# Where a mixture-of-experts stage sums its outputs: in the tokens themselves, or in two tiles of their own

## The chip, the core and the metric

The kernel runs on one core of a Trainium2 chip. The core has a matrix engine (PE, whose weight loads are shown apart as PEld), a vector engine (DVE), a scalar engine (ACT), a general one (POOL), and SP, which here issues nearly all DMAs. The metric is the time of one execution on the device in microseconds (us), as the median of several runs. A profile is one further execution, recorded by the hardware.

## The reference

Two encoder layers over 512 tokens of 1024 float32 values, each layer an attention block followed by a mixture of experts, and a final norm. The change lies in the mixture. Each of 16 experts picks its 64 best tokens by softmax affinity, runs a gated MLP over them, weighs its outputs with the affinity, and all outputs are added to the tokens from which they came:

```python
def expert_choice_ffn(xn, w_router, w_gate, w_up, w_down):
    aff = jax.nn.softmax((xn @ w_router).astype(jnp.float32), axis=-1)
    g, idx = lax.top_k(aff.swapaxes(1, 2), cap)          # cap = 64
    xs = xn[bidx, idx]
    hid = jax.nn.silu(jnp.einsum('becd,edf->becf', xs, w_gate)) * jnp.einsum('becd,edf->becf', xs, w_up)
    y = jnp.einsum('becf,efd->becd', hid, w_down) * g[..., None].astype(xn.dtype)
    return jnp.zeros_like(xn).at[bidx, idx].add(y)
...
        h = h + expert_choice_ffn(rms_norm(h, ffn_norm[l]), w_router[l], w_gate[l], w_up[l], w_down[l])
```

Every expert reads the tokens as they were before any expert's output was added. The result must therefore be summed somewhere while the unchanged tokens are still wanted.

## The kernel before, in words

The tokens stand in SBUF in two tiles h[0] and h[1] (columns 0 to 511 and 512 to 1023), four groups of 128 tokens each. The experts are worked off in eight pairs (e = 0, 2, ... 14), an expert of a pair on each half of the 128 output rows. For a pair the kernel:

- makes a one-hot matrix `oh` on DVE that says which token goes to which of 128 places (`one_hot`);
- gathers: PE multiplies the tokens with `oh`, which gives the pair's tokens already transposed, in eight blocks `k` of 128 columns. DVE evicts them times the norm's gain into `xs`;
- forms gate products (`og`, bank tag `in`), then up products (bank tag `S`), `expert_mm` at L1195; in the middle of the gate stage it also adds the half left over from the pair before (`rest`) and makes the affinities and the transposed one-hot matrix `G` (`places`);
- applies the gate, transposes the hidden values, forms the two halves of the down products (n = 0, 1), splits each half into a high and a low f32r part (`weighted`), and scatters it back through `G` (`combine`, L1364), whose result DVE adds into h (L1365).

The last three pairs (`tail` = 3) form only their first down half at once; the second halves come after pair 7, when the next layer's input products are already being mixed in.

Three devices keep the tokens readable in the kernel before. Pairs 0 and 1 gather from h itself (`gather`, L1223): exact f32 products of 128 columns. Pair 0's two down halves are not added to h but kept in a tile `hold` until pair 2 (`held`). After pair 1's gather h is split into an f32r high part `hh` and a low part `hl` (`token_parts`, ACT and POOL, four big tiles), and from these the later pairs gather in rounds (`gather_round`, L1236): pairs 2 and 3, 4 and 5, 6 and 7 together, 256 columns at a time, once with `hh` and once with `hl`. The first round stands before pair 2; the other two stand in pairs 3 and 5, around the transposes of the hidden values.

The order on PE in this stage is the order in which the code is written, since nearly all of its matmuls are `pinned`. DVE, ACT and POOL follow a scheduler. SP sends the weights in the order of use. All big tiles (tokens, parts, sums, held halves, gathered tokens of the rounds, weights `ew` of 1 MB each) come out of one pool of 25 buffers of 1 MB; a weight tile is sent when a buffer is free for it and the eighth DMA before it has landed.

Of the kernel before, what the change touches and what calls it, by code (L numbers as in the profile page):

```python
# [9 lines left out]
F32 = mybir.dt.float32  # L10
F32R = mybir.dt.float32r
# [5 lines left out]
P = 128  # L17
# [44 lines left out]
def build(tc, x, w_in, w_uq, w_ukv, w_out, w_gate, w_up, w_down, pv, wr, cst, nab, fin, out):  # L62
    nc = tc.nc
    ctx = ExitStack()
    with ctx:
# [303 lines left out]
        for L in range(DEPTH):  # L369
# [833 lines left out]
            ROUNDS = ((0,), (1,), (2, 3), (4, 5), (6, 7))  # L1203
            round_of = {pair: r for r in ROUNDS for pair in r}

            def token_parts(j):

                hh, hl = (big(n, F32R).rearrange("p (t d) -> p t d", t=NT) for n in ("hh", "hl"))
                for t in range(NT):
                    pinned(nc.scalar.activation(hh[:, t], h[j][:, t], AF.Copy))  # L1210
                    sub(nc.gpsimd, hl[:, t], h[j][:, t], hh[:, t])
                for x, part in zip(st.setdefault("parts", ([], [])), (hh, hl)):
                    x.append(part)
# [15 lines left out]
            def gather_round(oh, n, k0, m):  # L1229

                pg = p_t()[:, :m * n * P].rearrange("p (k s) -> p k s", k=m)
                for k in range(m):
                    cs = slice((k0 % 4 + k) * P, (k0 % 4 + k + 1) * P)
                    for t in range(NT):
                        for x in st["parts"]:
                            pinned(nc.tensor.matmul(pg[:, k], x[k0 // 4][:, t, cs], oh[:, t],  # L1236
                                                    start=(t == 0 and x is st["parts"][0]),
                                                    stop=(t == NT - 1 and x is st["parts"][1])))
                for i in range(n):
                    nc.vector.tensor_tensor(st["xs"][:, i, k0:k0 + m], pg[:, :, i * P:(i + 1) * P],  # L1240
                                            gains(k0, m), op=ALU.mult)

            def hidden(e, gate_w=(), up_w=(), ahead=None, before=None, then=None):
# [24 lines left out]
                if ahead:  # L1268
                    i = len(late)
                    if i % 4 == 0:  # L1270
                        st["G"] = big("G", F32R)
                    G = st["G"][:, i % 4 * 512:i % 4 * 512 + 512]
                else:

                    G = sm("qn" if pair in (1, 2) else "kn", F32R)

                def places():

                    pA = p_q()
                    for t in range(NT):  # L1280
                        pinned(nc.tensor.matmul(pA[:, :NEXP + 1], oh[:, t] if whole else oh[:, t].bitcast(F32),
                                                affr[:, t], start=(t == 0), stop=(t == NT - 1)))
# [6 lines left out]
                    nc.vector.tensor_copy(G, pG if whole else pG.bitcast(F32))  # L1289
# [24 lines left out]
                n = len(round_of.get(pair + 1, ())) if pair and pair == round_of[pair][-1] else 0  # L1314
                if n:
                    oh_n = one_hot(spool.tile([P, 2 * 512], F32R, name=nm("oh"), tag="oh", bufs=1), e + 2, 2 * n)
# [11 lines left out]
                def next_round(k0, k1):  # L1328
                    if k0 == 0:
                        st["xs"] = big("xs").rearrange("p (i k s) -> p i k s", i=2, k=KD)  # L1330
                    for k in range(k0, k1, 2):
                        gather_round(oh_n, n, k, 2)
                    if k1 == KD:
                        st["oh"] = oh_n
# [12 lines left out]
                if n and not whole:  # L1347
                    next_round(KD - 2, KD)
# [10 lines left out]
            def combine(n, y, G, banks, cs):  # L1359

                for t in range(NT):
# [3 lines left out]
                    nc.vector.tensor_tensor(h[n][:, t, cs], h[n][:, t, cs], o, op=ALU.add)  # L1365

            def half_then(n, ws, G, asl, hT, before=None, bank=p_s, banks=(p_q, p_t, p_t, p_o), cs=slice(0, 512),
                          held=False):
# [6 lines left out]
                if held:  # L1375
                    if n == 0:
                        st["hold"] = big("hold")
                    y = st["hold"][:, n * 512:(n + 1) * 512]
                    act(y, oy, asl)

                    def later():

                        yh, yl = sm("sb", F32R), sm("sb", F32R)
                        act(yh, y)
                        sub(nc.vector, yl, y, yh)
                        return lambda: combine(n, (yh, yl), G, banks, cs)
                    return later
# [3 lines left out]
            gate_w, rest, held = gate0, None, []  # L1391
            for e in range(0, NEXP - 2 * tail, 2):
                then = None
                if e == 4:
                    def then():
                        held.pop(0)()()
                p = hidden(e, gate_w, up0 if e == 0 else (), before=rest, then=then)
                down_w = down0 if e == 0 else [down_half(e, n) for n in range(2)]
                gate_w = [weights(w_gate, 2, k, 2) for k in range(0, KD, 2)] if e == 0 else ()
                if e == 0:  # L1400
                    held += [half_then(n, down_w[n], *p, held=True) for n in range(2)]
                    continue
                if e == 2:
                    token_parts(0)
                rest = half_then(0, down_w[0], *p, held.pop(0)() if e == 4 else None)
                if e == 2:
                    token_parts(1)
                rest = half_then(1, down_w[1], *p, rest)
                if e == 2:
                    st["gather"]()  # L1410
# [194 lines left out]
```

## Time and profile before

| | us |
|---|---|
| median of 3 runs | 1532.53 (1530.0 to 1533.62) |
| the profiled execution, its own time | 1528.89 |
| its span in the profile | 1527.1 |
| PE busy | 1444.4 (95%) |
| PE weight loads busy | 854.5 (56%) |
| DVE busy | 598.1 (39%) |
| ACT busy | 367.4 (24%) |
| POOL busy | 237.7 (16%) |

The span is what the profile covers of the execution's own time; 1.8 us lie around it. An f32 product stands in the records as two matmuls, an f32r product as one. A matmul's end in the records is modelled and lies behind the start of the next one, so what a piece of PE's work takes is read from start to start. Layer 0's first gather starts at 307.12, layer 1's at 1065.02.

### The profile page before, as it was taken

The numbers are of one execution on the slowest core, as the hardware profiler recorded it, in microseconds if no ns is written. First come the engines' busy times: TensorE is split into PE (matmuls) and PEld (weight loads), VectorE is DVE, ScalarE is ACT, GpSimd is POOL, SyncE is SP. The second block draws the span as 40 slices with busy tenths as digits, with TensorE's granted clock in tenths as the row PEclk, the third lists the DMA queues.
The fourth block names the chain that finished last, engine by engine and source line by source line (L and its number), as shares of the span: only waits on it lengthen the run. The fifth ranks groups of instructions, "written<-read, shape, count | busy, mean of one in ns | idle before, by whom it ended". The sixth has DMA issues, their size and how long they took to land.

```text
span 1527.1 us, 21209 instructions
## 1 busy us (share of the span) xinstructions
PE 1444.4 (95%) x8262; PEld 854.5 (56%) x8262; DVE 598.1 (39%) x1519; ACT 367.4 (24%) x949; POOL 237.7 (16%) x339
## 2 busy tenths in 40 slices
PE   9999899999999999987999998998999999999886
PEld 8987777644444433532489877675444434344323
DVE  6767675710223212210376577657102222221113
ACT  4434645300200000001134346452101000000002
POOL 3532442000200000000124235320002000000002
PEclk9999999999999999999999999999999999999998
DMA  6122263789999999999811123547899999999995
GB/s 202 51 71 78 70 203 139 303 327 414 376 415 421 421 421 421 421 421 418 342 56 44 52 77 111 163 192 300 341 380 409 417 420 420 421 421 422 421 421 232
DMA packets 80436, 444.99 MB, mean 291 GB/s; under 512 B 7761, under 2 KB 23633, under 8 KB 32465
## 3 DMA queue, kind: packets, MB, share of 16 engines
q1 hardware_dynamic: 76688, 438.40, 72.0%
q0 software_dynamic: 3648, 5.24, 1.6%
q8 instruction: 65, 1.06, 0.3%
q14 instruction: 35, 0.28, 0.1%
HBM read 436.28 MB, written 2.10 MB: 287 GB/s over the span
## 4 chain that ended last, share of the span: by engine, by line
PE 76%; DMA 15%; DVE 6%; ACT 2%; issue 1%; POOL 0%; DVEq 0%; SPq 0%; ACTq 0%; POOLq 0%
PE S L1195 19%; PE in L1195 14%; DMA ew<-in_w_gate_dram 5%; DMA ew<-in_w_up_dram 5%; PE in L161 5%; PE in L163 5%; PE in L162 5%; PE tr L155 5%; PE o L297 4%; DMA ew<-in_w_down_dram 4%; PE tr L1236 2%; PE tr L1223 2%; PE tr L1364 2%; PE trq L1364 1%; PE trq L1009 1%
## 5 line engine op out<-in xcount | busy, mean ns | idle before, releaser
L1195 PE MATMUL S<-ew,PT 128*64 128x512 f32 x960 | 214.0, 595 | 2.4 <-DMA ew<-in_w_down_dram 2.4
L1195 PE MATMUL S<-ew,xs 128*64 128x512 f32 x768 | 173.3, 594 | 11.9 <-DMA ew<-in_w_up_dram 11.9
L1195 PE MATMUL in<-ew,xs 128*64 128x512 f32 x768 | 172.6, 595 | 5.9 <-DMA ew<-in_w_gate_dram 5.9
L1321 DVE SCALAR_TENSOR_TENSOR sb<-S,rsl,sb 128x512 f32<-128x512 f32 x32 | 24.0, 751 | 302.2 <-PE S L1195 302.2
L1195 PEld LDWEIGHTS S<-ew,PT 128*64 128x64 f32 x960 | 67.1, 137 | 133.2 <-issue 127.2
L1195 PEld LDWEIGHTS S<-ew,xs 128*64 128x64 f32 x768 | 56.7, 137 | 126.5 <-issue 100.4
L1195 PEld LDWEIGHTS in<-ew,xs 128*64 128x64 f32 x768 | 54.3, 137 | 109.3 <-issue 97.0
L146 POOL TENSOR_SCALAR wh<-wraw 128x384 fp32r<-128x384 f32 (+2 forms) x40 | 36.9, 942 | 360.0 <-DMA ew<-in_w_down_dram 300.0
L1310 ACT ACTIVATE sb<-in,rsl 128x512 f32<-128x512 f32 x32 | 21.8, 687 | 245.5 <-PE in L1195 198.1
L161 PE MATMUL in<-wh,hT 128*128 128x256 f32 (+1 forms) x256 | 77.6, 304 | 0.3 <-ACT cut L143 0.3
L162 PE MATMUL in<-wl,hT 128*128 128x256 f32 (+1 forms) x256 | 77.6, 303 | 0.0
L163 PE MATMUL in<-wh,hT 128*128 128x256 f32 (+1 forms) x256 | 77.4, 303 | 0.0
L1195 PE MATMUL in<-ew,PT 128*64 128x512 f32 (+1 forms) x352 | 73.9, 559 | 0.0
L1365 DVE TENSOR_TENSOR h<-h,trq 128x512 f32<-128x512 f32 (+1 forms) x31 | 20.8, 671 | 130.2 <-PE trq L1364 130.2
L155 PE MATMUL tr<-c,sb 128*128 128x128 f32 x324 | 55.1, 284 | 7.5 <-DVE sb L1321 4.2
L1345 ACT ACTIVATE PT<-tr 128x512 f32<-128x512 f32 x24 | 14.3, 597 | 187.6 <-PE tr L155 187.6
L146 POOL TENSOR_SCALAR sb<-sb,cut 128x512 f32<-128x512 f32 (+2 forms) x64 | 43.0, 672 | 95.6 <-DVE cut L576 44.5
L1471 POOL TENSOR_TENSOR fo<-h,fg 128x512 f32<-128x512 f32 x4 | 5.0, 1280 | 337.9 <-DMA fg<-in_fin_dram 337.9
L146 POOL TENSOR_SCALAR cut<-cut,cut 128x512 f32<-128x512 f32 (+2 forms) x64 | 42.2, 660 | 74.5 <-DVE cut L576 44.0
L149 DVE SCALAR_TENSOR_TENSOR sb<-S,asl,sb 128x512 fp32r<-128x512 f32 x18 | 13.5, 751 | 102.2 <-ACT sb L143 102.2
L152 POOL TENSOR_TENSOR hl<-h,hh 128x512 fp32r<-128x512 f32 x16 | 20.0, 1276 | 211.2 <-ACT hh L1210 211.2
L155 PEld LDWEIGHTS tr<-c,sb 128*128 128x128 f32 x324 | 36.4, 143 | 28.3 <-issue 16.2
(392 smaller groups left out, 2783.5 us busy)
## 6 DMA issues: line engine op xcount, KB each, us to landing
ew<-in_w_up_dram SPq DMA_DIRECT2D x128, 1024.0 KB, 16.9
ew<-in_w_down_dram SPq DMA_DIRECT2D x124, 1024.0 KB, 17.6
ew<-in_w_gate_dram SPq DMA_DIRECT2D x120, 1024.0 KB, 17.6
wraw<-in_w_in_dram SPq DMA_DIRECT2D x8, 1024.0 KB, 8.9
ew<-in_w_gate_dram SPq DMA_DIRECT2D x16, 512.0 KB, 9.9
woraw<-in_w_out_dram SPq DMA_DIRECT2D x6, 1024.0 KB, 4.9
nab<-in_nab_dram SPq DMA_DIRECT2D x4, 896.0 KB, 4.6
wraw<-in_w_in_dram SPq DMA_DIRECT2D x4, 832.0 KB, 4.7
```

Source lines behind the costliest of these rows:

```text
L146: nc.gpsimd.tensor_scalar(o, i, r, 1.0, op0=ALU.mult, op1=ALU.mult)
L155: return nc.tensor.transpose(o, i, ident)
L161: nc.tensor.matmul(o, lh, rh, start=start, stop=False)
L162: nc.tensor.matmul(o, lh, rl, start=False, stop=False)
L163: nc.tensor.matmul(o, ll, rh, start=False, stop=stop)
L297: nc.tensor.matmul(o[a * 64:(a + 1) * 64, :], v_of(a, kb), PTs[a][:, i * P:(i + 1) * P], start=(i == 0), stop=(i == len(kbs) - 1))
L1195: pinned(nc.tensor.matmul(o[n][a * 64:(a + 1) * 64, :], src[k // 4][:, k % 4, a * 64:(a + 1) * 64], ws[a][:, k - k0, n * 512:n * 512 + o[n ...
L1223: pinned(nc.tensor.matmul(pg[:, k], h[k0 // 4][:, t, (k0 % 4 + k) * P:(k0 % 4 + k + 1) * P], oh[:, t], start=(t == 0), stop=(t == NT - 1)))
L1236: pinned(nc.tensor.matmul(pg[:, k], x[k0 // 4][:, t, cs], oh[:, t], start=(t == 0 and x is st["parts"][0]), stop=(t == NT - 1 and x is st[ ...
L1310: nc.scalar.activation(s, og[n], AF.Silu, scale=rsl)
L1321: nc.vector.scalar_tensor_tensor(sg[j], ou, rsl, sg[j], op0=ALU.mult, op1=ALU.mult)
L1364: pinned(nc.tensor.matmul(o, G[:, t * P:(t + 1) * P], y[j], start=(j == 0), stop=(j == 1)))
```

## The change

The outputs of all experts are summed in two tiles of their own, `acc`, and h stays as it is until every pair has gathered. Every pair then gathers from h as pairs 0 and 1 did, four times two blocks, in its own gate stage. The first combine of each group of tokens is a copy into `acc` and no add. In pair 7, behind its gate products in the code, `add_up` adds `acc` to h in eight steps, half of them on DVE and half on POOL; what is combined after that is added to h. The token parts, the rounds, the held halves and the tile `xs` of the rounds go. `places` stands in the middle of the gate stage in pair 1 too.

```diff
-            ROUNDS = ((0,), (1,), (2, 3), (4, 5), (6, 7))
-            round_of = {pair: r for r in ROUNDS for pair in r}
-            def token_parts(j):
-                hh, hl = (big(n, F32R).rearrange("p (t d) -> p t d", t=NT) for n in ("hh", "hl"))
-                for t in range(NT):
-                    pinned(nc.scalar.activation(hh[:, t], h[j][:, t], AF.Copy))
-                    sub(nc.gpsimd, hl[:, t], h[j][:, t], hh[:, t])
...
+            acc = []
+            st["sum"] = None
...
-            def gather_round(oh, n, k0, m):
-                pg = p_t()[:, :m * n * P].rearrange("p (k s) -> p k s", k=m)
-                for k in range(m):
-                    cs = slice((k0 % 4 + k) * P, (k0 % 4 + k + 1) * P)
...
-                            pinned(nc.tensor.matmul(pg[:, k], x[k0 // 4][:, t, cs], oh[:, t],
...
+            def add_up():
+                for n in range(2):
                     for t in range(NT):
+                        eng = nc.vector if (n * NT + t) % 4 < 2 else nc.gpsimd
+                        eng.tensor_tensor(h[n][:, t], h[n][:, t], acc[n][:, t], op=ALU.add)
+                st["sum"] = h
...
-                whole = pair < 2
-                if whole:
-                    oh, xs = one_hot(sm("qn"), e, 2) if e else oh0, []
-                else:
-                    i2 = round_of[pair].index(pair)
-                    oh = st["oh"][:, :, i2 * P:(i2 + 1) * P]
-                    xs = [st["xs"][:, i2, j * 4:j * 4 + 4] for j in range(2)]
+                oh, xs = one_hot(sm("qn"), e, 2) if e else oh0, []
                 og = [p_in(), p_in()]
-                steps = [KN["st"], [2, 2, 2, 2]][pair] if whole else []
+                steps = [2, 2, 2, 2] if pair else KN["st"]
...
-                    pG = p_t(F32 if whole else F32R)
+                    pG = p_t()
                     for t in range(NT):
-                        pinned((T32 if whole else TR)(pG[:, t * P:(t + 1) * P], oh[:, t]))
+                        pinned(T32(pG[:, t * P:(t + 1) * P], oh[:, t]))
...
-                i_places = n_gate - 1 if pair == 1 else n_gate // 2 - 1
...
-                    if i == i_places:
+                    if i == n_gate // 2 - 1:
                         if before:
                             before()
                         places()
-                    if i == n_gate // 2 and then:
-                        then()
+                if e == NEXP - 2:
+                    add_up()
...
-                if n and not whole:
-                    next_round(0, KD - 2)
-                st["gather"] = lambda: next_round(0, KD)
                 hT = []
...
-                if n and not whole:
-                    next_round(KD - 2, KD)
                 return G, asl, hT
...
-                    nc.vector.tensor_tensor(h[n][:, t, cs], h[n][:, t, cs], o, op=ALU.add)
+                    if len(acc) == n:
+                        acc.append(big("sum").rearrange("p (t d) -> p t d", t=NT))
+                    y_ = (st["sum"] or acc)[n][:, t, cs]
+                    if (n, t) in first_sums:
+                        first_sums.remove((n, t))
+                        nc.vector.tensor_copy(y_, o)
+                    else:
+                        nc.vector.tensor_tensor(y_, y_, o, op=ALU.add)
...
-                if e == 0:
-                    held += [half_then(n, down_w[n], *p, held=True) for n in range(2)]
-                    continue
-                if e == 2:
-                    token_parts(0)
-                rest = half_then(0, down_w[0], *p, held.pop(0)() if e == 4 else None)
-                if e == 2:
-                    token_parts(1)
+                rest = half_then(0, down_w[0], *p)
                 rest = half_then(1, down_w[1], *p, rest)
-                if e == 2:
-                    st["gather"]()
```

On PE, at the start of pair 3 in layer 0, the last down products of pair 2 (tag `S`) stand directly before pair 3's gate products (tag `in`) in the kernel before:

```order
L1195 MATMUL S_4085<-ew_4042,PT_4026 64x512
L1195 MATMUL in_4122<-ew_4127,xs_3778 64x512 [waits DMAHW6_49]
L1195 MATMUL in_4122<-ew_4129,xs_3778 64x512 [waits DMAHW7_49]
L1195 MATMUL in_4123<-ew_4127,xs_3778 64x512
L1195 MATMUL in_4123<-ew_4129,xs_3778 64x512
```

In the changed kernel, at the same place, two of the four steps of pair 3's gather (L1214, the former L1223) come between, and the gate products wait for DVE's eviction of the first:

```order
L1195 MATMUL S_4027<-ew_4004,PT_3988 64x512
L1214 MATMUL tr_4076<-qn_4064,h_70 128x128 [waits DVE_49]
L1214 MATMUL tr_4076<-qn_4064,h_70 128x128 x7
L1214 MATMUL tr_4087<-qn_4064,h_70 128x128 [waits DVE_49]
L1214 MATMUL tr_4087<-qn_4064,h_70 128x128 x7
L1195 MATMUL in_4067<-ew_4072,PT_4085 64x512 [waits DMAHW6_49,DVE_49]
L1195 MATMUL in_4067<-ew_4074,PT_4085 64x512 [waits DMAHW7_49]
L1195 MATMUL in_4068<-ew_4072,PT_4085 64x512
```

So 16 gather products moved in front of the gate; the other 16 stand between its pieces.

On PE, later in pair 3, the transposes of the hidden values (L155) have the second round's products (L1236) on both sides in the kernel before:

```order
L1236 MATMUL tr_4305<-oh_4209,hh_3731 128x256
L1236 MATMUL tr_4305<-oh_4209,hl_3732 128x256
L155 MATMUL tr_4324<-c,sb_4205 128x128 [waits DVE_49,PE_49]
L155 MATMUL tr_4324<-c,sb_4205 128x128 x3
L155 MATMUL tr_4331<-c,sb_4207 128x128 [waits DVE_49,PE_49]
L155 MATMUL tr_4331<-c,sb_4207 128x128 x3
L1236 MATMUL tr_4338<-oh_4209,hh_3731 128x256 [waits Activation_49]
L1236 MATMUL tr_4338<-oh_4209,hl_3732 128x256
```

In the changed kernel the up products go before them and the down products (`S_4278`) behind them:

```order
L1195 MATMUL S_4222<-ew_4229,PT_4118 64x512
L155 MATMUL tr_4248<-c,sb_4192 128x128 [waits DVE_49]
L155 MATMUL tr_4248<-c,sb_4192 128x128 x3
L155 MATMUL tr_4255<-c,sb_4194 128x128 [waits DVE_49]
L155 MATMUL tr_4255<-c,sb_4194 128x128 x3
L1195 MATMUL S_4278<-ew_4262,PT_4253 64x512 [waits DMAHW6_49,Activation_49]
L1195 MATMUL S_4278<-ew_4264,PT_4253 64x512 [waits DMAHW7_49]
```

The 64 products of the round are gone from here, as are those of the two other rounds.

On DVE, in pair 7's gate stage of layer 0, the combine's adds into h are followed by the affinities (`asl`, `rsl`) and G (`kn`) and then by the gate itself in the kernel before:

```order
L1365 TENSOR_TENSOR h_70<-h_70,tr_5145 128x512 [waits PE_49]
L1365 TENSOR_TENSOR h_70<-h_70,o_5149 128x512 [waits PE_49]
L1284 COPY asl_5118<-trq_5153 64x1 [waits PE_49]
L1284 COPY asl_5118<-trq_5153 64x1
L1285 COPY rsl_5119<-trq_5153 128x1
L1289 CAST kn_5120<-tr_5161 128x512 [waits PE_49]
L1321 SCALAR_TENSOR_TENSOR sb_5183<-S_5188,rsl_5119,sb_5183 128x512 [waits PE_49,Activation_49]
```

In the changed kernel the combine adds into `sum`, four adds of `add_up` (L1225) stand among these, and the eviction of pair 7's last gather step (L1218) stands behind them all:

```order
L1332 TENSOR_TENSOR sum_3509<-sum_3509,tr_5134 128x512 [waits PE_49]
L1225 TENSOR_TENSOR h_70<-h_70,sum_3509 128x512 [waits DVE_49]
L1332 TENSOR_TENSOR sum_3509<-sum_3509,tr_5138 128x512 [waits PE_49]
L1332 TENSOR_TENSOR sum_3509<-sum_3509,o_5142 128x512 [waits PE_49]
L1225 TENSOR_TENSOR h_70<-h_70,sum_3509 128x512 [waits DVE_49]
L1262 COPY asl_5079<-trq_5146 64x1 [waits PE_49]
L1262 COPY asl_5079<-trq_5146 64x1
L1263 COPY rsl_5080<-trq_5146 128x1
L1267 CAST kn_5081<-tr_5154 128x512 [waits PE_49]
L1225 TENSOR_TENSOR h_71<-h_71,sum_3594 128x512 [waits PE_49] x2
L1218 TENSOR_TENSOR PT_5120<-tr_5160,pvt 128x256 [waits PE_49]
L1294 SCALAR_TENSOR_TENSOR sb_5194<-S_5199,rsl_5080,sb_5194 128x512 [waits PE_49,Activation_49]
```

The adds were put ahead of an eviction for which the gate's last products wait; SP's DMAs are the same in number and order.

## Rows read from the trace of the kernel before

**Rows 1.** The page: busy tenths of PE and of DMA in 40 slices.
```profile
PE   9999899999999999987999998998999999999886
...
DMA  6122263789999999999811123547899999999995
```

**Rows 2.** PE's waits, whole span: us in total, times, longest.
```profile
PE S L1195 <- DMA ew<-in_w_up_dram: 11.9, 12, 1.4
PE in L1195 <- DMA ew<-in_w_gate_dram: 5.9, 4, 1.9
...
PE S L1195 <- DMA ew<-in_w_down_dram: 3.0, 5, 1.3
```

**Rows 3.** Windows: span; PE, PEld, DVE, ACT, POOL busy; clock, DMA, GB/s.
```profile
320.00:340.00 20.00, 20.00 (x102) 7.90 (x102) 2.77 (x7) 2.66 (x3) 0.00 (x0) 1.00 0.85 334
...
380.00:400.00 20.00, 19.64 (x100) 7.55 (x98) 2.63 (x6) 2.91 (x6) 0.00 (x0) 1.00 0.82 321
...
700.00:720.00 20.00, 15.39 (x68) 4.92 (x64) 1.50 (x2) 1.20 (x2) 1.95 (x4) 1.00 1.02 417
```

**Rows 4.** PE's timeline, layer 0, pair 1: start, us, instruction, records.
```profile
359.90 3.84 PE L1223 MATMUL tr<-qn,h 128*128 128x128 f32 x32
...
381.82 1.06 PE L1281 MATMUL trq<-aff,qn 128*128 128x17 f32 x8
382.73 0.64 PE L155 MATMUL tr<-c,qn 128*128 128x128 f32 x4
```

**Rows 5.** PE's timeline, first round and pair 2's gate, layer 0.
```profile
414.86 0.39 PE L1236 MATMUL tr<-oh,hh 128*128 128x256 f32 x1
...
422.72 7.09 PE L1195 MATMUL in<-ew,xs 128*64 128x512 f32 x32
...
432.52 0.51 PE L158 MATMUL tr<-ident_r,oh 128*128 128x128 f32 x4
```

**Rows 6.** PE's timeline, pairs 2 to 7 of layer 0.
```profile
442.07 13.90 PE L1195 MATMUL S<-ew,xs 128*64 128x512 f32 x64
...
457.51 3.65 PE L1195 MATMUL S<-ew,PT 128*64 128x512 f32 x16
...
492.79 13.90 PE L1195 MATMUL S<-ew,xs 128*64 128x512 f32 x64
...
516.03 10.52 PE L1195 MATMUL S<-ew,PT 128*64 128x512 f32 x48
...
621.25 7.09 PE L1195 MATMUL S<-ew,hk 128*64 128x512 f32 x32
628.17 7.04 PE L1195 MATMUL in<-ew,xs 128*64 128x512 f32 x32
635.13 0.74 PE L1364 MATMUL trq<-sb,G 128*128 128x512 f32 x2
...
638.37 7.09 PE L1195 MATMUL in<-ew,xs 128*64 128x512 f32 x32
645.28 7.89 PE L1195 MATMUL S<-ew,xs 128*64 128x512 f32 x34
...
729.12 0.73 PE L1364 MATMUL trq<-sb,kn 128*128 128x512 f32 x2
```

**Rows 7.** PE's timeline, pairs 6 and 7 of layer 1.
```profile
1402.81 7.89 PE L1195 MATMUL S<-ew,xs 128*64 128x512 f32 x34
...
1484.88 0.72 PE L1364 MATMUL trq<-sb,kn 128*128 128x512 f32 x2
...
1486.92 7.96 PE L1195 MATMUL in<-ew,hk 128*64 128x512 f32 x32
```

**Rows 8.** Lines 152 and 1365: durations in ns, min/median/max; starts; shapes.
```profile
L152 DVE TENSOR_TENSOR Cl<-cut,Ch x6: 686/711/1528, 81.6 to 890.1; 128x512 fp32r<-128x512 f32 x6
...
L152 POOL TENSOR_TENSOR hl<-h,hh x16: 1262/1277/1295, 400.1 to 1168.9; 128x512 fp32r<-128x512 f32 x16
...
L1365 DVE TENSOR_TENSOR h<-h,trq x31: 420/689/691, 410.1 to 1512.8; 128x512 f32<-128x512 f32 x29, 128x256 f32<-128x256 f32 x2
```

More of the change, by code (lines that the diff above doesn't have):

```diff
@@ L1227, in gather, with hidden @@
                 nc.vector.tensor_tensor(xs[k0 // 4][:, k0 % 4:k0 % 4 + n], pg, gains(k0, n), op=ALU.mult)
-            def gather_round(oh, n, k0, m):
-                pg = p_t()[:, :m * n * P].rearrange("p (k s) -> p k s", k=m)
-                for k in range(m):
-                    cs = slice((k0 % 4 + k) * P, (k0 % 4 + k + 1) * P)
+            def add_up():
+                for n in range(2):
                     for t in range(NT):
-                        for x in st["parts"]:
-                            pinned(nc.tensor.matmul(pg[:, k], x[k0 // 4][:, t, cs], oh[:, t],
[L1237 to L1243, printed above, removed]
-                pair = e // 2
-                whole = pair < 2
-                if whole:
-                    oh, xs = one_hot(sm("qn"), e, 2) if e else oh0, []
-                else:
-                    i2 = round_of[pair].index(pair)
-                    oh = st["oh"][:, :, i2 * P:(i2 + 1) * P]
-                    xs = [st["xs"][:, i2, j * 4:j * 4 + 4] for j in range(2)]
+                        eng = nc.vector if (n * NT + t) % 4 < 2 else nc.gpsimd
+                        eng.tensor_tensor(h[n][:, t], h[n][:, t], acc[n][:, t], op=ALU.add)
+                st["sum"] = h
+            def hidden(e, gate_w=(), up_w=(), ahead=None, before=None):
+                pair = e // 2
+                oh, xs = one_hot(sm("qn"), e, 2) if e else oh0, []
                 og = [p_in(), p_in()]
-                steps = [KN["st"], [2, 2, 2, 2]][pair] if whole else []
+                steps = [2, 2, 2, 2] if pair else KN["st"]
                 k0s = [sum(steps[:i]) for i in range(len(steps))]
@@ L1273, in hidden @@
                 else:
-                    G = sm("qn" if pair in (1, 2) else "kn", F32R)
+                    G = sm("kn", F32R)
                 def places():
@@ L1280, in places @@
                     for t in range(NT):
-                        pinned(nc.tensor.matmul(pA[:, :NEXP + 1], oh[:, t] if whole else oh[:, t].bitcast(F32),
+                        pinned(nc.tensor.matmul(pA[:, :NEXP + 1], oh[:, t],
                                                 affr[:, t], start=(t == 0), stop=(t == NT - 1)))
@@ L1364, in combine, with half_then @@
                         pinned(nc.tensor.matmul(o, G[:, t * P:(t + 1) * P], y[j], start=(j == 0), stop=(j == 1)))
[L1365 to L1368 removed]
+                    if len(acc) == n:
[6 more added lines that the diff above has]
+                        nc.vector.tensor_tensor(y_, y_, o, op=ALU.add)
+            first_sums = [(n, t) for n in range(2) for t in range(NT)]
+            def half_then(n, ws, G, asl, hT, before=None, bank=p_s, banks=(p_q, p_t, p_t, p_o), cs=slice(0, 512)):
                 oy = bank()[:, :cs.stop - cs.start]
@@ L1374, in half_then @@
                         before()
[L1375 to L1387, printed above, removed]
                 y = weighted(oy, asl)
                 return lambda: combine(n, y, G, banks, cs)
-            gate_w, rest, held = gate0, None, []
+            gate_w, rest = gate0, None
             for e in range(0, NEXP - 2 * tail, 2):
[L1393 to L1397, printed above, removed]
+                p = hidden(e, gate_w, up0 if e == 0 else (), before=rest)
                 down_w = down0 if e == 0 else [down_half(e, n) for n in range(2)]
                 gate_w = [weights(w_gate, 2, k, 2) for k in range(0, KD, 2)] if e == 0 else ()
-                if e == 0:
-                    held += [half_then(n, down_w[n], *p, held=True) for n in range(2)]
-                    continue
-                if e == 2:
-                    token_parts(0)
-                rest = half_then(0, down_w[0], *p, held.pop(0)() if e == 4 else None)
-                if e == 2:
-                    token_parts(1)
+                rest = half_then(0, down_w[0], *p)
                 rest = half_then(1, down_w[1], *p, rest)
-                if e == 2:
-                    st["gather"]()
             gate_w = ()
```

14 lines of the change are left out of this document (1 added, 13 removed).

## Prediction

> **What bounds the kernel now.** I read the share of each engine and the 40 slices first: in most of both expert stages (slices 10 to 19 and 30 to 39) PE and the DMA engines are full together [rows 1]. So the next question is which of them waits for the other. PE's waits answer it: the largest are for expert weights, 20.8 us in the three rows [rows 2], while nothing else in the expert stages comes near. The windows say when: the stream of weights has holes early in the stage (DMA share 0.85 at 320:340, 0.82 at 380:400: 3.0 + 3.6 = 6.6 us of DMA time unused), while at 700:720 it is full at 417 GB/s and PE is busy only 15.39 of 20 us [rows 3]. PE runs through a pair of experts faster than its weights arrive; it starts the stage with weights in hand, has used them up by pair 6's up products, and from there waits for tile after tile. The end of a layer's stage is therefore PE's work plus these late waits, and a change in PE's work must first fill them before it costs anything.
>
> **PE's work: six gathers in place of three rounds, per layer.** The new kernel gathers pairs 2 to 7 as pairs 0 and 1 are gathered now, by exact f32 products of 128 columns, one pair at a time; the old one gathered 256 columns (two pairs) at once from two f32r parts.
> - A pair's gather: in pair 1 the gate stage with its gather runs from 359.90 to 381.82 = 21.92 us [rows 4]. The gate products alone take 6.96 (628.17 to 635.13) + 6.91 (638.37 to 645.28) = 13.87 [rows 6]. So a gather costs 8.05 us; six are 48.3. From below, the row of 32 records (half a gather) is 3.84 long [rows 4]: 7.7 a pair, 46.1 for six.
> - A round: the one after pair 1 stands alone on PE from 414.86 to 422.72 = 7.86 [rows 5]. The one in pair 3 is seen in the time from the start of the up products to that of the down products: 516.03 - 492.79 = 23.24, against 457.51 - 442.07 = 15.44 in pair 2, which has none: 7.80 [rows 6]. With the one in pair 5 taken like it, three are 23.5.
> - Net: 48.3 - 23.5 = 24.8 us more PE work a layer, 49.7 in both.
> - G's transposes become f32: 0.64 instead of 0.51 for four [rows 4, 5], in six pairs of two layers at most 1.6; much of such a length is the tail of the last one, so I take 0.6.
>
> **What that fills.** In layer 0 PE goes from pair 6's up products at 645.28 to the combine at 729.12 in 83.84 us [rows 6]. The work between is two ups with their transposes (2 x 15.44), two down halves (621.25 to 628.17, 2 x 6.92), a gate (13.87), a combine with the places (635.13 to 638.37, 3.24) and half a down half (3.46): 65.3. The other 18.5 us are waiting. The same piece of layer 1 takes 1484.88 - 1402.81 = 82.07, so 16.8, and 0.9 more in the next 32 records (7.96 against 7.04) [rows 6, 7]. In sum 36.2, more than the waits listed, because a matmul's modelled end hides part of a gap.
>
> These waits go if the tiles come no later than now. At pair 6's up products the new PE is 5 x 8.05 - 23.5 = 16.8 us later; at 729.12, after the waits that it no longer has, 24.8 - 18.5 = 6.3 us later. So every tile that is late now would be early by 6 us or more. The stream itself has no reason to be later: SP issues the same DMAs in the same order; a tile is sent when an older one's buffer is free, and where PE frees buffers later it has that many tiles in hand; and of 25 big buffers two go to the sums, where now four go to the token parts, one to the held halves and one or two to the gathered tokens.
>
> **The other edits.** The held halves and their late split move ACT's and DVE's work, not PE's: the number of combines is the same. The token parts' eight ACT copies and eight POOL subtractions a layer go, under cover now. New are eight adds in pair 7: four on DVE (a 128x512 of two SBUF inputs has a median of 0.71) and four on POOL (1.28) [rows 8]. They stand on DVE behind the combine's adds (0.69 each) and ahead of the last gather's eviction, and PE needs that for the last quarter of the gate. PE's cover is 3.24 + 2.0 (a quarter gather) + 3.5 (a quarter gate) = 8.7 us from the combine's start; DVE needs 0.6 + 4 x 0.69 + 4 x 0.71 + 1.0 (G and the small copies, an estimate from the 0.69 row) + 0.4 = 7.6. So nothing; without that cover, up to 2.5 us a layer (two POOL adds of 1.28 waited for). The rows allow it: the longest of six such DVE instructions took 1.53, the shortest 0.69 [rows 8]. I take 0 and keep 5 us for the upper end. The Trainium skill's page "SBUF — State Buffer" (section "Who interferes with whom") says that a DVE instruction with two SBUF inputs and a GpSimd one that reads SBUF exclude each other, and the later one waits out the other. That speaks against splitting these adds over the two engines; the 1.53 agrees with it, and by the rule the sum below would be some 3 us higher.
>
> At the start of a pair DVE now has the last half's low part ahead of the first eviction. PE gathers a second quarter meanwhile, so I cost it at nothing; the last rival below prices it.
>
> **Sum.** 49.7 + 0.6 - 36.2 = +14.1 us. Against the profiled execution's own 1528.9 that is 1543.0. The profiled one is 3.6 us below the median of the runs, 1532.5, and I forecast the median: 1546.
>
> **Rivals.**
> - DMA stays the bound and hides it all: 1532. For it: DMA at 1.02 of its share and PE short of tiles [rows 3]. Against: the waits to fill are 18.5 us in layer 0, the extra work is 24.8; it needs gathers of at most (23.5 + 18.5) / 6 = 7.0 us, and the row says 8.05.
> - Faster: the freed buffers close the holes in the stream, which then ends 6.6 us earlier in each layer: 1532.5 - 13.2 = 1519. It decides only while DMA is the bound, so while a gather costs at most (23.5 + 18.5 - 6.6) / 6 = 5.9 us. The pace of the only such gathers in the trace speaks against it: 32 records from 359.90 in 3.84 [rows 4] are 0.12 us each, and a pair has 64. The Trainium skill's "TensorE: Matmul & The Clock Gate" (section "Back-to-back issue gap") gives a sustained 81 ns for a matmul of 128 columns beside its weight load; by it a pair would take 64 x 0.081 = 5.2 us, an estimate, and this rival would win. The trace does not agree.
> - The waits stay: the stream is delayed along with PE, and nothing is filled: 1532.5 + 50.3 = 1583. For it only that some SP waits are for PE's buffers; against it the free buffers above.
> - A new wait at each pair's start: evictions queue behind the low part of the last half, 0.7 us on ACT and 0.7 on DVE, in seven pairs of two layers: up to 20 us more, 1566. It decides if the second quarter of the gather, 1.9 us, doesn't cover them.
>
> **How the numbers follow.** The forecast has 0.80, hidden 0.07, faster 0.04, waits stay 0.04, new wait 0.05. From below the forecast loses 4.4 us with gathers of 7.7, and the runs scatter by 2.5: 1538. From above: if only the listed waits go, 50.3 - 20.8 = 29.5 makes 1562, and the adds' 5 us come on top; I cut at 1558, where about half of that is left. Outside lie most of the rivals, 0.18. Within 0.2% (3 us, about what a measurement of this kernel tells from no change) lies the hidden case and a little of the forecast: 0.08. Faster 0.05, slower 0.87.
>
> **What would show it.** Right: PE's rows for waits on expert weights vanish; each of pairs 1 to 7 shows 64 gather records of 8 us in its gate stage; PE passes pair 6's up products with the DMA queue still some 15 us ahead, and layer 0's last combine ends some 6 us later than now. The forecast falls if PE still waits for weights at pair 7, if gathers of the later pairs run quicker than pair 1's, or if PE waits for DVE's evictions at the start of a gate.

## The result, and the profile after

The changed kernel takes 1541.43 us (median of 4 runs, 1539.48 to 1545.39), the kernel before 1531.38 in the same session (4 runs, 1530.00 to 1533.62): 1.0072 times as long, 95% interval 1.0047 to 1.0097. So it is slower, by 10 us; 14 were forecast. The profiled execution took 1539.48 us with a span of 1537.7, which is 10.6 more than the span before.

One of the four runs of light_before below took 3617.41 us and the others 1491.96 to 1493.80; what is said of it goes by those three.

The page's slices of PE and DMA, to be held against [rows 1]: PE is now full to the end of both expert stages. The last slice of layer 0's stream (the 20th digit of DMA) is a 6 where it was an 8, and the last of the span a 3 where it was a 5.

```profile
PE   9999899899999999999999998998999999999996
...
DMA  6122264789999999999610124557899999999993
```

A slice of the longer span lies later, so these digits alone don't show an earlier stream. The rows of the queue that sends the weights (SPq) do: pair 6's up tiles and the last 16 weight tiles of layer 0's experts are sent from 618.59 and 690.79 us on after, and from 620.70 and 693.60 before. First before, then after:

```profile
620.70 18.11 SPq L1166 DMA_DIRECT2D ew<-in_w_up_dram  x8
...
693.60 37.26 SPq L1166 DMA_DIRECT2D ew<-in_w_down_dram  x16
```

```profile
618.59 17.84 SPq L1166 DMA_DIRECT2D ew<-in_w_up_dram  x8
...
690.79 37.29 SPq L1166 DMA_DIRECT2D ew<-in_w_down_dram  x16
```

PE's waits for expert weights before are the three rows of [rows 2] and this fourth one, 23.5 us together (us in total, times, longest):

```profile
PE in L1195 <- DMA ew<-in_w_down_dram: 2.7, 2, 1.4
```

After, no row for expert weights is left in the whole span; the largest are for DVE.

```profile
PE tr L155 <- DVE sb L1294: 5.8, 16, 0.4
PE in L161 <- DVE un L149: 5.4, 3, 2.5
```

The windows that answer to [rows 3]. At 700:720 PE is busy 19.97 of 20 us (15.39 before) beside a stream as full as then, and the second hole of the stream, at 380:400, is nearly closed: 0.96 for 0.82.

```profile
320.00:340.00 20.00, 20.00 (x107) 8.63 (x108) 2.99 (x8) 2.66 (x3) 0.00 (x0) 1.00 0.84 320
380.00:400.00 20.00, 20.00 (x99) 7.36 (x100) 2.12 (x5) 1.38 (x2) 0.00 (x0) 1.00 0.96 393
700.00:720.00 20.00, 19.97 (x101) 7.83 (x102) 6.32 (x10) 2.66 (x3) 6.32 (x4) 1.00 1.02 415
```

PE's timeline in pair 2 of layer 0 (start, us, instruction, records), which answers to [rows 4, 5]: three gather rows of 32, 16 and 16 records, 64 together, between pieces of the gate.

```profile
419.57 3.84 PE L1214 MATMUL tr<-qn,h 128*128 128x128 f32 x32
423.34 3.65 PE L1195 MATMUL in<-ew,PT 128*64 128x512 f32 x16
426.92 2.05 PE L1214 MATMUL tr<-qn,h 128*128 128x128 f32 x16
428.90 3.65 PE L1195 MATMUL in<-ew,PT 128*64 128x512 f32 x16
432.49 0.73 PE L1324 MATMUL trq<-sb,kn 128*128 128x512 f32 x2
...
435.72 1.95 PE L1214 MATMUL tr<-qn,h 128*128 128x128 f32 x16
437.60 7.09 PE L1195 MATMUL in<-ew,PT 128*64 128x512 f32 x32
444.52 1.89 PE L1195 MATMUL S<-ew,PT 128*64 128x512 f32 x8
```

By their starts the gather rows are 3.77 + 1.98 + 1.88 = 7.63 us long and the gate's pieces 3.58 + 3.59 + 6.92 = 14.09. Pairs 1 to 6 of both layers run like this one.

The marks that answer to [rows 6, 7]: the first gather of each layer, pair 6's up products, and pair 7's combine.

```profile
661.30 1.03 PE L1195 MATMUL S<-ew,PT 128*64 128x512 f32 x4
...
735.02 0.73 PE L1324 MATMUL trq<-sb,kn 128*128 128x512 f32 x2
...
1071.02 2.05 PE L1214 MATMUL tr<-qn,h 128*128 128x128 f32 x16 [0.72 <-DVE qn L1126]
...
1424.18 1.03 PE L1195 MATMUL S<-ew,PT 128*64 128x512 f32 x4
...
1497.90 0.73 PE L1324 MATMUL trq<-sb,kn 128*128 128x512 f32 x2
```

In what follows a "stage" is the time from a layer's first gather to pair 7's combine, the piece that the change touches. Before, layer 0's began here, so it was 729.12 - 307.12 = 422.00 us long:

```profile
307.12 2.05 PE L1223 MATMUL tr<-qn,h 128*128 128x128 f32 x16 [0.73 <-DVE qn L1126]
```

Layer 1's began at 1065.02: 419.86. After, the first gather of layer 0 starts at 308.14, and both stages are 426.88 us long to the hundredth. The span's 10.6 us are then: start +1.0, stage of layer 0 +4.9, from there to layer 1's first gather +0.1 (335.90 and 336.00), stage of layer 1 +7.0, from its end to the last combine -0.9, behind that -1.5.

### The profile page after: what moved, and what is told of

It reads as the page before. It is cut to its first block, busy times and chain, and to the rows that moved or that the text cites. A ratio compares the mean times of both kernels' runs of the same rounds, so it can differ in the third digit from the quotient of the medians.

```text
span 1537.7 us, 21939 instructions
## 1 busy us (share of the span) xinstructions
PE 1480.5 (96%) x8646; PEld 890.9 (58%) x8646; DVE 606.9 (39%) x1527; ACT 356.4 (23%) x929; POOL 230.3 (15%) x331
## 4 chain that ended last, share of the span: by engine, by line
PE 87%; DMA 5%; DVE 5%; ACT 2%; issue 1%; POOL 0%; DVEq 0%; POOLq 0%; ACTq 0%; SPq 0%
PE S L1195 25%; PE in L1195 16%; PE tr L1214 8%; PE tr L155 5%; PE in L161 5%; PE in L163 5%; PE in L162 5%; PE o L297 4%; DMA ew<-in_w_down_dram 2%; PE tr L1324 2%; DMA ew<-in_w_up_dram 1%; PE trq L1324 1%; DMA mq<-mq 1%; PE trq L1009 1%; PE trq L1259 1%
## 5 line engine op out<-in xcount | busy, mean ns | idle before, releaser
L1195 PE MATMUL S<-ew,PT 128*64 128x512 f32 x1728 | 378.4, 593 | 0.0
L1195 PEld LDWEIGHTS S<-ew,PT 128*64 128x64 f32 x1728 | 121.8, 137 | 240.0 <-issue 237.4
L1195 PE MATMUL in<-ew,PT 128*64 128x512 f32 (+1 forms) x1120 | 247.1, 585 | 0.1
L1195 PEld LDWEIGHTS in<-ew,PT 128*64 128x64 f32 x1120 | 75.4, 136 | 131.8 <-issue 121.9
L1214 PEld LDWEIGHTS tr<-qn,h 128*128 128x128 f32 x1024 | 118.1, 192 | 28.7 <-issue 26.0
L1225 POOL TENSOR_TENSOR h<-h,sum 128x512 f32<-128x512 f32 x8 | 12.6, 1608 | 806.1 <-DVE sum L1332 806.1
L1214 PE MATMUL tr<-qn,h 128*128 128x128 f32 x1024 | 126.2, 279 | 1.4 <-DVE qn L1126 1.4
L1218 DVE TENSOR_TENSOR PT<-tr,pvt 128x256 f32<-128x256 f32 (+1 forms) x66 | 27.5, 416 | 129.1 <-PE tr L1214 129.1
L155 PE MATMUL tr<-c,sb 128*128 128x128 f32 x324 | 54.9, 284 | 6.5 <-DVE sb L1294 5.8
L155 PEld LDWEIGHTS tr<-c,sb 128*128 128x128 f32 x324 | 36.1, 143 | 30.3 <-issue 18.3
L143 ACT ACTIVATE sb<-S,asl 128x512 fp32r<-128x512 f32 x22 | 15.1, 688 | 161.1 <-PE S L1195 161.1
L162 PEld LDWEIGHTS in<-wl,hT 128*128 128x128 f32 x256 | 48.6, 190 | 0.3 <-issue 0.2
L161 PEld LDWEIGHTS in<-wh,hT 128*128 128x128 f32 x256 | 48.5, 190 | 0.4 <-issue 0.2
```

What stands on the lines that cost most here:

```text
L155: return nc.tensor.transpose(o, i, ident)
L161: nc.tensor.matmul(o, lh, rh, start=start, stop=False)
L162: nc.tensor.matmul(o, lh, rl, start=False, stop=False)
L1195: pinned(nc.tensor.matmul(o[n][a * 64:(a + 1) * 64, :], src[k // 4][:, k % 4, a * 64:(a + 1) * 64], ws[a][:, k - k0, n * 512:n * 512 + o[n ...
L1214: pinned(nc.tensor.matmul(pg[:, k], h[k0 // 4][:, t, (k0 % 4 + k) * P:(k0 % 4 + k + 1) * P], oh[:, t], start=(t == 0), stop=(t == NT - 1)))
L1218: nc.vector.tensor_tensor(xs[k0 // 4][:, k0 % 4:k0 % 4 + n], pg, gains(k0, n), op=ALU.mult)
```

## The experiments

All times are in one table. Stages and waits are read from one profiled execution each, the medians from several runs, but for the last two kernels, which ran once. The kernel before had a median of 1530.40 us beside light_before, light_after, half_gather and wide, 1530.67 beside half_held, parts, two_rounds and late_round, and 1531.76 in one run beside the last two. Waits are PE's listed waits for expert weights, in both layers. In the code cuts "..." stands for lines left out, and the comments are added.

| kernel | stage 0, us | stage 1, us | waits, us | median, us | against before, 95% |
|---|---|---|---|---|---|
| before | 422.00 | 419.86 | 23.5 | 1531.38 | |
| after | 426.88 | 426.88 | 0 | 1541.43 | 1.0047 to 1.0097 |
| light_before | 403.13 | 403.15 | 0 | 1492.45 | 0.9709 to 0.9786 |
| light_after | 426.88 | 426.88 | 0 | 1536.91 | 1.0015 to 1.0051 |
| half_gather | 418.28 | 416.37 | 14.0 | 1521.13 | 0.9913 to 0.9964 |
| half_held | 425.23 | 423.06 | 22.5 | 1534.83 | 1.0015 to 1.0041 |
| parts | 428.57 | 425.51 | 32.0 | 1543.44 | 1.0060 to 1.0097 |
| wide | 424.14 | 422.28 | 1.3 | 1535.97 | 1.0013 to 1.0049 |
| two_rounds | 422.41 | 417.75 | 12.2 | 1530.30 | 0.9982 to 1.0007 |
| late_round | 418.50 | 418.54 | 0 | 1525.71 | 0.9955 to 0.9981 |
| adds_pool | 426.46 | 426.47 | 0 | 1544.97 | |
| adds_dve | 426.78 | 426.77 | 0 | 1543.45 | |

The time between the stages is 332 to 343 us long in these traces, though no edit changes its products; stages tell the kernels apart more sharply than whole runs do.

**Without the stream: light_before and light_after.** The same edit in both kernels:

```diff
-nc.sync.dma_start(wt, w_[L, e + a, k0 // n].rearrange("p (k n) -> p k n", k=n))
-ws.append(wt)
+nc.sync.dma_start(wt[:, :n // 2], w_[L, e + a, k0 // n].rearrange("p (k n) -> p k n", k=n)[:, :n // 2])
+ws.append(wt[:, :n // 2])
...
-        ws[a][:, k - k0, n * 512:n * 512 + o[n].shape[1]],
+        ws[a][:, (k - k0) % ws[a].shape[1], n * 512:n * 512 + o[n].shape[1]],
```

(and the same halving for up and down). light_before:

> The kernel before, with half of the bytes of the experts' weights: of each tile only the first half of its blocks is loaded, and the products use them twice (PE's work is unchanged, the output is not the reference's; the first pair's four mixed gate tiles stay whole). Theory: the late waits on weights are the stream's and amount to 36.2 us in both layers, so without them the kernel takes 1531 - 36 = 1495 us (1491 to 1500), and the combine of pair 7 in layer 0 stands some 18.5 us earlier. Rival A: only the listed waits (20.8 us) are the stream's: 1510. Rival B: PE waits there for something else than the stream: 1531.

light_after:

> The changed kernel with the same halved stream of experts' weights (output not the reference's). Theory: its PE waits for no weights, so a lighter stream gives back nothing: 1540 to 1542 us, and without the stream the change costs its whole PE work, 2 x (6 x 7.84 - 23.5) = 47 us plus 0.9 for the sums' adds: light_after minus light_before is 44 to 50 us where the full kernels differ by 10. Rival A: the changed kernel is still bound by its stream in part, with the waits hidden in the modelled ends of the products: some 10 us are given back, 1531. Rival B: the gathers are cheaper than they look (7.0 us each): the two light kernels differ by 37.

The marks of layer 0, light_before first:

```profile
309.21 2.05 PE L1223 MATMUL tr<-qn,h 128*128 128x128 f32 x16 [0.72 <-DVE qn L1126]
...
712.34 0.73 PE L1364 MATMUL trq<-sb,kn 128*128 128x512 f32 x2
```

light_after:

```profile
309.36 1.83 PE L1214 MATMUL tr<-qn,h 128*128 128x128 f32 x14 [0.73 <-DVE qn L1126]
...
736.24 0.73 PE L1324 MATMUL trq<-sb,kn 128*128 128x512 f32 x2
```

light_before came out at 1492.45, as the theory had it. Its stages are 18.87 and 16.71 us shorter than before's: that is what the stream cost, 35.6 us, where the forecast had 18.5 + 16.8. Rivals A and B are out. light_after's stages are 426.88 us, the same as with the full stream to the hundredth: behind the first gather the changed kernel loses nothing to its weights. With a stream too light to wait for, the change costs 426.88 - 403.14 = 23.74 us a layer. In whole runs the two differ by 44.5, at the low end of the 44 to 50 expected. light_after itself, 1536.91, is 3 us below its range: it is 4.5 below the changed kernel, all outside the stages (in the traces 332.1 us between them for 336.0), which I hadn't expected.

**Half of the new PE work: half_gather.**

```diff
-    for t in range(NT):
+    for t in range(ts):
...
-gather(oh, xs, k0s[done], steps[done])
+gather(oh, xs, k0s[done], steps[done], NT if pair < 2 else NT // 2)   # token blocks contracted
```

> The changed kernel, but pairs 2 to 7 gather over the first two of the four token blocks only, so that each of their gathers costs 3.9 us in place of 7.8 (the output is not the reference's): PE's work a layer is then 6 x 3.9 = 23.5 us, the same as the three rounds of the kernel before. Theory: PE is ahead of the stream again, the waits on weights at pairs 5 to 7 come back, and the stream sets the end; it gave back 10 of the 47 us and not more. As the sums take fewer buffers than the token parts did and the stream ran some 3 us a layer earlier in the changed kernel (DMA share 0.79 against 0.92 at 740:760), 1522 to 1529, 1525 the likeliest. Rival A: PE alone sets the time: 1541 - 47 = 1494. Rival B: free buffers bring the stream nothing: 1531, as before.

PE's waits of this kernel:

```profile
PE S L1195 <- DMA ew<-in_w_up_dram: 8.4, 8, 1.3
...
PE S L1195 <- DMA ew<-in_w_down_dram: 3.0, 5, 1.3
...
PE in L1195 <- DMA ew<-in_w_down_dram: 2.6, 2, 1.3
```

1521.13: 0.9 below the theory's range of 1522 to 1529, and far from rival A's 1494. The waits are back, so the stages show the stream's floor, the shortest stage that the stream allows, with the changed kernel's buffers: 418.28 and 416.37, which is 3.7 and 3.5 below before. Rival B is out: the freed buffers do bring the stream forward. The changed kernel stands 8.6 and 10.5 us above its floor.

**The buffers by themselves: half_held.**

```diff
+if e == 2:
+    kept_ = [big("kept") for _ in range(4)]        # read again in pair 5
+    for b in kept_:
+        nc.gpsimd.memset(b[:, :1], 0.0)
...
```

> half_gather with four big buffers taken out of the pool from pair 1 to pair 5, which is where the token parts stood in the kernel before (one column of each is written, and added to a scale as zero in pair 5; gathers halved as there). Theory: the 3.6 us by which half_gather's stages were shorter than those of the kernel before (418.3 against 422.0, 416.4 against 419.9) came from the freed buffers: with four taken away the stages are 421 to 426 us and the time 1527 to 1535, and the early hole in the stream (380:400) is back. Rival: buffers are not what the stream waited for: 1521 as half_gather.

Window 380:400, half_gather and then half_held:

```profile
380.00:400.00 20.00, 20.00 (x106) 8.37 (x107) 3.55 (x10) 1.37 (x2) 0.00 (x0) 1.00 0.96 387
```

```profile
380.00:400.00 20.00, 20.00 (x96) 6.71 (x96) 1.84 (x4) 1.38 (x2) 0.29 (x3) 1.00 0.65 250
```

The hole is back (DMA share 0.65 for 0.96), and the stages are 7.0 and 6.7 us longer: 1.7 us a stage for each of the four big buffers, on average. Shown, as expected.

**One part of the change alone: parts.** The sums in their own tiles, the gathers in rounds from token parts as before, no held sums. Against the changed kernel, without the lines of the parts and rounds themselves, which are those of the kernel before:

```diff
...
+if e == 2:
+    token_parts(0)
 rest = half_then(0, down_w[0], *p)
+if e == 2:
+    token_parts(1)
 rest = half_then(1, down_w[1], *p, rest)
+if e == 2:
+    st["gather"]()
```

> One part of the change alone: the outputs are summed in two tiles of their own and no sums are held, but pairs 2 to 7 gather in the three f32r rounds of the kernel before, from the token parts. Theory: PE's work is that of the kernel before again (403 us from the first gather to pair 7's combine, and 0.4 for the sums' adds), the stream sets the end, and with two sums in place of one held buffer the stage is 422 to 425 us long in place of 420 to 422: 1531 to 1537, 1533 the likeliest; waits on weights at pairs 5 to 7 are back. Rival A: it is the sums that cost the 10 us: 1541. Rival B: dropping the held sums saves time: under 1528.

```profile
380.00:400.00 20.00, 20.00 (x96) 6.74 (x96) 1.18 (x2) 1.38 (x2) 0.00 (x0) 1.00 0.47 186
```

A miss: 1543.44, 6 above my range and no better than the whole change. Rival A named the time but not the reason: PE is hardly busier (2.5 and 1.3 us a stage), it waits 32.0 us for weights, and the stream has a deeper hole at 380:400 (0.47 for 0.82 before: 7.0 us more of unused DMA time, about what the stages lost, 6.6 and 5.7). Sums and parts held together cost 6 us a layer of stream. I had counted one buffer more than before. After pair 2, when the held tile is free again, it is two; but the stage is nearly as much longer as four cost in half_held, and which of the tiles make up the rest isn't settled.

**Two pairs in one exact gather: wide.** f32 products of 256 columns from the unchanged tokens, in three rounds.

```diff
...
+for t in range(NT):
+    pinned(nc.tensor.matmul(pg[:, k], h[k0 // 4][:, t, cs], oh[:, t],   # oh: 2 pairs, 256 columns
+                            start=(t == 0), stop=(t == NT - 1)))
...
```

> The changed kernel, but pairs 2 to 7 gather two pairs at once, in exact f32 products of 256 columns from the unchanged tokens, in three rounds that stand where the rounds of the kernel before stood (one more big buffer for the gathered tokens). Theory: 64 records of 0.22 us a round, 14.1 us, against 2 x 7.84 for two gathers: 4.8 us a layer less PE work, 1541 - 9.6 = 1532 (1529 to 1535), still without waits on weights at pair 7. Rival A: the records go at twice the pace of those with 128 columns, 2 x 0.1225 = 0.245, 15.7 a round: 1541. Rival B: the round in a piece lets PE wait for DVE or hands the weights' buffers on later, 2 us each round: 1541 + 2 to 1544.

```profile
419.58 14.08 PE L1228 MATMUL tr<-oh,h 128*128 128x256 f32 x64
433.59 0.65 PE L1195 MATMUL in<-ew,xs 128*64 128x512 f32 x2
```

A round takes 14.01 us, as the theory said, and stage 1 is 4.6 us shorter than after's. Stage 0 is 2.7 shorter, with a wait on weights at its end (1.3 us): the stream has holes again, DMA share 0.84 at 380:400 and 0.90 at 420:440 for 0.96 and 1.01 in the changed kernel. I take them to come from the gathered tokens' buffer; no run tests that alone. 1535.97 is 1 above the range.

**Where the sums' adds run: adds_pool and adds_dve** (one profiled run each).

```diff
-eng = nc.vector if (n * NT + t) % 4 < 2 else nc.gpsimd
-eng.tensor_tensor(h[n][:, t], h[n][:, t], acc[n][:, t], op=ALU.add)
+nc.gpsimd.tensor_tensor(h[n][:, t], h[n][:, t], acc[n][:, t], op=ALU.add)    # adds_dve: nc.vector
```

> The changed kernel with all eight adds of the sums on POOL in place of four on DVE and four on POOL. Theory: the adds that ran beside each other slowed each other (DVE 0.68 alone and up to 1.76 beside POOL, POOL 1.27 and 1.72), and that is what made pair 7's gate stage 25.37 us instead of 24.94; alone on POOL each takes 1.27 to 1.30, DVE is free for the gather's last eviction, and pair 7's gate stage is 24.94 again in both layers; the time is 0.9 us less, within the scatter. Rival: POOL's adds are slow for another reason (1.7 us each still), or pair 7's stage stays at 25.37.

> The changed kernel with all eight adds of the sums on DVE. Theory: each takes 0.68 with nothing beside it, but twelve of these, the small copies (0.5), G's (0.68) and the eviction (0.41) are 9.8 us from DVE's first add, against 7.2 us after which PE wants the last quarter's tokens: PE waits 2 to 3 us in pair 7 of each layer, whose gate stage is 27 to 28 us. Rival: the eviction is not held up by the adds, 24.9 to 25.4.

First the changed kernel itself, DVE, POOL and PE's weight loads in pair 7 of layer 0:

```profile
698.65 0.68 DVE L1225 TENSOR_TENSOR h<-h,sum 128x512 f32<-128x512 f32 x1
...
700.45 1.45 DVE L1225 TENSOR_TENSOR h<-h,sum 128x512 f32<-128x512 f32 x1
...
702.83 2.43 DVE L1225 TENSOR_TENSOR h<-h,sum 128x512 f32<-128x512 f32 x2
705.19 0.41 DVE L1218 TENSOR_TENSOR PT<-tr,pvt 128x256 f32<-128x256 f32 x1
...
700.08 6.32 POOL L1225 TENSOR_TENSOR h<-h,sum 128x512 f32<-128x512 f32 x4 [403.58 <-DVE sum L1332]
...
705.65 0.20 PEld L1195 LDWEIGHTS in<-ew,PT 128*64 128x64 f32 x4 [0.91 <-DVE PT L1218]
```

DVE's add takes 0.68 while POOL is idle and up to 1.76 beside it; POOL's four take 6.32. The last eviction of the gather comes at 705.19, and PE's weight load waits 0.91 us for it (such gaps are 0.28 elsewhere). Pair 7's gate stage, 683.76 to 709.13, is 25.37 us long against 24.94 in pair 6. In adds_pool (duration in ns, min/median/max) all sixteen are quick, and pair 7's gate stage is 24.94 and 24.95 in the two layers, the stages 426.46 and 426.47:

```profile
L1224 POOL TENSOR_TENSOR h<-h,sum x16: 1257/1262/1279, 698.8 to 1475.6; 128x512 f32<-128x512 f32 x16
```

So the two engines' adds slow each other, and splitting them costs 0.43 us a layer. The times of these single runs, 1544.97 and 1543.45, can't show that much. adds_dve went the rival's way, 25.26 in both layers and not 27 to 28: alone each add takes 0.68 and starts 0.60 after the last, and the last of the eight stands behind the eviction in DVE's order, so that it is late by less than I had worked out. adds_pool also takes DVE's adds from in front of the eviction; but in adds_dve seven quick adds stand there and cost 0.32, so four quick ones, 3 x 0.60 = 1.8 us sooner, would cost nothing (an estimate), and I put the 0.43 down to the slowing. adds_dve's DVE rows:

```profile
700.72 3.09 DVE L1224 TENSOR_TENSOR h<-h,sum 128x512 f32<-128x512 f32 x5
703.73 0.41 DVE L1218 TENSOR_TENSOR PT<-tr,pvt 128x256 f32<-128x256 f32 x1
704.06 0.68 DVE L1224 TENSOR_TENSOR h<-h,sum 128x512 f32<-128x512 f32 x1
```

**A version between the two: two_rounds and late_round.** Sums in their own tiles and whole gathers first; the parts are made late, and the last pairs gather in rounds. In the changed kernel the queue that issues the weights waits for PE's buffers 35 us of 40 at 380:420 and 2.8 at 620:660, so four buffers taken there should cost the stream little.

```diff
...
-ROUNDS = ((0,), (1,), (2, 3), (4, 5), (6, 7))        # of parts
+ROUNDS = ((0,), (1,), (2,), (3,), (4,), (5,), (6, 7))  # late_round; two_rounds: (4, 5), (6, 7)
...
 nxt["gate"] = [weights(w_gate, e + 2, k, 2) for k in range(0, KD, 2)]
+if e == 10:                                            # late_round: parts in pair 5; two_rounds: in pair 3
+    token_parts(0)
+    token_parts(1)
...
```

> Sums in tiles of their own; pairs 0 to 3 gather whole from the unchanged tokens, and the parts are made in pair 3 for two f32r rounds, (4,5) and (6,7). Theory: PE's work in a stage is 426.9 - 2 x 7.85 = 411.2 us, below the 416 to 418 at which the stream set the end in half_gather, so the stream is the bound; the four buffers of the parts are taken at some 530 us, where the queue still waits for PE's buffers for 9 us of 40: the stream comes some 5 us later, stages of 421 to 423: 1530 to 1534. Rival A: the buffers are free by then: 1521 to 1526. Rival B: all four are missed, 4 x 2.45 us a layer: 1540.

> As two_rounds, but pairs 0 to 5 gather whole, the parts are made in pair 5, and only pairs 6 and 7 gather in a round. Theory: PE's work in a stage is 426.9 - 7.85 = 419.0 us and stays the bound or level with the stream; at 640 us the queue waits for PE's buffers for 3 us of 40, so the parts' buffers cost the stream 2 us or less: 419 to 421 a stage, 1541 - 2 x 7 = 1527 (1525 to 1530), which would be faster than both kernels. Rival A: the parts' POOL work, 8 x 1.28 us, is not done when PE reaches the round and PE waits 3 to 5 us a layer for it: 1534 to 1537. Rival B: four buffers missed, 9.8 us of stream a layer of which 8 are PE's lead: 1530 to 1534.

late_round, layer 0's marks and the start of its round:

```profile
306.80 1.38 PE L1225 MATMUL tr<-qn,h 128*128 128x128 f32 x10 [0.72 <-DVE qn L1126]
...
627.94 7.09 PE L1195 MATMUL S<-ew,hk 128*64 128x512 f32 x32
634.95 0.39 PE L1238 MATMUL tr<-oh,hh 128*128 128x256 f32 x1
...
725.30 0.73 PE L1371 MATMUL trq<-sb,kn 128*128 128x512 f32 x2
```

The round starts with no wait, so POOL had the parts in time (rival A is out), and no wait on weights is left (rival B is out). Its stages are 418.50 and 418.54, PE's own work and within 2.2 us of the stream's floor. 1525.71 us is 0.32% faster than before (0.19 to 0.45), and faster than the changed kernel. two_rounds frees PE further than the stream can follow: 12.2 us of waits, and no difference from before; its second stage, 417.75, is shorter than the 421 to 423 expected.

## Why the prediction was right, and where its size was off

- **The bound.** Right. PE's late waits were the stream's, and the change fills them: light_before gives 35.6 us in the stages and 0.9 behind them (28.20 to 27.32 from pair 7's combine to the last one in layer 1), 36.5 against the forecast's 36.2. The listed waits, 23.5, are too few, as the prediction said they would be.
- **PE's work.** The mechanism is right, and this is the term that was mis-sized: 49.7 + 0.6 us was forecast, 2 x 23.74 = 47.5 was measured, with 0.9 of it from the sums' adds, which had no part in that term. Without them it is 46.6, so 3.7 less than forecast. Of these 2.5 are the gathers: each was taken as 21.92 - 13.87 = 8.05 us, and cost 24.95 - 3.24 - 13.87 = 7.84, which is 7.63 in its own rows and 0.22 for cutting the gate (14.09 for 13.87). Pair 1 before, from which the 21.92 was read, has the places behind the gate and not in its middle, and two rows that stand next to other products there are 0.1 us longer: the third gather row (372.82 to 374.80, 1.98 for 1.88) and the gate's last piece (374.80 to 381.82, 7.02 for 6.92). The 0.6 for G's transposes shows in no row: combine and places take 3.23 us in pair 2 after (432.49 to 435.72), and took 3.24. The last 0.6 is spread over rows of a few tenths, of both signs, where the order of combines and places changed. In sum, 3.7 less for this term, 0.9 more for the adds and 0.3 less for the waits are the 3.1 us by which the stages and the tail behind them, +11.0, fall short of the forecast's +14.1; that the adds' miss stands against the gathers' is luck.
- **The stream is not later.** Right, and more: it is earlier, by 3.7 and 3.5 us of floor (half_gather), since sums take fewer buffers than parts (half_held). That is the faster rival's mechanism, with half of its 6.6 us, and it didn't decide because PE is the bound: the rival wanted gathers of 5.9 us. The pace of the gather rows is 7.63 us for 64, 0.12 each; the 81 ns of the Trainium skill's "TensorE: Matmul & The Clock Gate" (section "Back-to-back issue gap") don't hold for these products after the change either.
- **The marks.** Pair 6's up products are 16.0 us later (16.8 forecast), pair 7's combine 5.9 (6.3), 1.0 of each from the later start. The queue sends pair 6's up tiles 2.1 us sooner, so it stands 18 us further ahead of these products than before, where PE waited for these tiles (some 15 forecast). Layer 0's last combine is 8.7 later and not 6: the next layer's first products stand between the last pairs' in another order (43.40 us for 40.56 from pair 7's combine on), and layer 1's attention took 2.7 us less. I have no experiment on that; the two cancel.
- **add_up at nothing.** Wrong, by 0.43 us a layer. The Trainium skill's "SBUF — State Buffer" (section "Who interferes with whom") spoke against the split, and the trace agrees that the adds slow each other, by up to 1.76 - 0.68 = 1.08 us, less than the other's whole 1.26, which doesn't settle whether one waits the other out; of the 3 us that the rule would add 0.9 came.
- **Start of a pair.** Right: PE has no row of waiting for a gather's evictions there, and its weight loads have only the two 0.91 us of pair 7.
- **Outside the stages** +1.0, +0.1 and -1.5 us were not forecast. They nearly cancel, and they are no larger than what such pieces differ by in kernels that don't touch them.

## What to carry to other kernels

Where a stream sets the end, the waits of the engine behind it are a budget: extra work costs only what exceeds it, and halving the bytes while keeping the products measures it. Work and buffers have to be priced together: four tiles held early in the stage delayed the stream here by 7 us, while late_round, which takes four once the queue hardly waits for buffers any more, shows no wait on weights and is faster than both kernels. To price a piece of work that cuts another, take its own rows and what the cut costs the other (7.63 + 0.22 here), and see whether the window it is read from ends between the same neighbours.

## What the runs showed of the hardware

- Two f32 adds of 128x512 from SBUF, one on DVE and one on POOL, slow each other: 0.68 and 1.26 us alone, up to 1.76 and 1.72 together.
- A record of an exact f32 gather costs 0.119 us with 128 columns (64 in 7.63) and 0.219 with 256 (64 in 14.01): doubling the columns saves only some 8% of the time.
- A stage in which PE waits for no weights repeats within 0.04 us between the layers (426.88 in both layers of after and of light_after, with half of the stream's bytes; 403.13 and 403.15 in light_before, 418.50 and 418.54 in late_round).
